# Silu as one activation in place, and the last four transposes of x into halves of two large buffers

## The chip, the cores and the metric

One core of a Trainium2 chip runs the whole program. TensorE (PE) multiplies, VectorE (DVE) and ScalarE (ACT) do the elementwise work, GpSimd (POOL) does almost nothing here, and SyncE (SP) issues nearly all transfers. The metric is the device time of one execution in microseconds (us), lower is better. Three executions of the kernel before give a median of 1471.03 us (1471.02 to 1471.4). The profiled execution took 1471.17 us, of which 1469.4 us lie between its first and its last instruction (the span).

## The reference, cut to what matters

Two decoder layers work on 512 tokens of width 1024, all in f32. One layer is:

```
h = rmsnorm(x);  z = h @ w_in
aq, ak, av, rq, rk, rv, rg, ga, gb = split(z)
ya = sliding_window_attention(aq, ak, av) @ w_a
r  = chunkwise_retention(rq, rk, rv)
r  = r * rsqrt(mean(r * r) + eps)
yb = (r * silu(rg)) @ w_b
x  = x + (sigmoid(ga) * ya + sigmoid(gb) * yb) @ w_out
x  = x + square(relu(rmsnorm(x) @ w_up)) @ w_down
```

A last rmsnorm of x, with its own gain, is the output. Two places of it matter below: silu(rg) = rg * sigmoid(rg), the gate of the retention, and the last `w_down` product with the norm behind it, where the kernel needs x with tokens instead of features on the partitions.

## The kernel before

**Tiling.** x lies in SBUF as eight tiles of 128 features by 512 tokens. Every f32 operand of a product is split into a high and a low part, and a product is three matmuls (hi*hi, hi*lo, lo*hi; `products`, L326), or fewer where two are put side by side. Weights arrive in 336 units of 128x1024 f32 (512 KB) in a fixed order (`unit_order`, L59). SP loads a unit into one of three `raw` buffers (L196), ScalarE writes its high part (L286) and VectorE the low part (L287), into three `hi` and three `lo` buffers. `unit` (L292) has the splits of the next units traced before the products of the present one, so weights are prepared about two units ahead. The last four units of the program go to homes of their own (`homes`, L270 and L525), because they are used until the end.

**Buffers.** Short-lived f32 tiles of 128x512 come from `temp` (L143), with six buffers for all of them. Larger ones of 128x2x512 come from `big` (L146), with seven. A tile waits until one of the buffers of its kind is given back.

**Order.** The Python code traces operations in program order; on leaving its context (L1662) a planner sets each engine's final order once, at build time: it runs a model of the timeline and gives a free engine the first traced operation whose inputs, buffers and semaphores are ready in the model. On the chip each engine, and SP's list of transfers, then runs strictly in that order and waits where something is late. `tc.issue_after(ins)` only keeps the operations in its block behind `ins` on the same engine.

**The retention's gates.** In each layer the eight tiles of rg are `w_in` chunks. `put_rg` (L982) takes a chunk out of PSUM with VectorE, times the norm's factor (L989), into half of a big tile `z`. Then `silu` (L995): ScalarE writes sigmoid(rg) to a temp `sig` (L997), VectorE multiplies it into rg (L998). For tiles 0 to 3 this comes in a block behind the last exponential of the attention, together with two sigmoids on half of the gates ga each (L1141 to L1145); for tiles 4 to 7 it comes from `put_rg` itself (L990). The eight gates gb follow as further chunks (`gate`, L920), with a sigmoid each (L923), while in the background the retention of heads 2 and 3 runs, whose norms take square roots (L454, and L479 for head 3). A head's `finish` (L1084) multiplies z with the norm and with the retention's output.

**The end.** In the last layer, x is turned by `turns` (L509): for each half f of the features, four transposes on VectorE (L516) write a temp `turned` each, SP sends each to DRAM (`blocks`, L517), and after the fourth, four transfers bring x back in the other layout (L520). For f=0 they are spread over the last `w_down` pairs of the third quarter (L1462). For f=1 they stand at the start of `end` (L540), behind the two gain rows `gains`, which hold two of the six temps to the end, and behind two big tiles `x0` for the output. There the products of the last quarter come in two parts. First four banks of PSUM take four units (L548 to L555). Then, for each block of 128 tokens, ScalarE seeds a bank with the turned x of f=1 (`seeded`, L560, copy on L562), TensorE adds the last four units' products on top (L573 to L578), and the norm and the store of that block follow (L579 to L597).

Of the kernel before, what the change touches and what calls it, by code (L numbers as in the profile page):

```python
# [13 lines left out]
AF = mybir.ActivationFunctionType  # L14
ALU = mybir.AluOpType
# [112 lines left out]
def decoder(ctx, tc, xT, x_first, w_in, w_a, w_b, w_out, w_up, w_down, tables, decay, band, triangles, g_last, out):  # L128
    nc = tc.nc
# [13 lines left out]
    def temp(name="t"):  # L143
        return tmp.tile([P, T], F32, tag="t", name=name)

    def big(name, dtype=F32):  # L146
        return tmp.tile([P, 2, T], dtype, tag="big", name=name, bufs=7)
# [361 lines left out]
    def turns(f):  # L509

        four = x[:, 4 * f : 4 * f + 4, :]

        def turn(n):
            new = temp("turned")
            old = four.rearrange("p c (b r j) -> p c b r j", b=NB, j=32)[:, :, :, n, :]
            nc.vector.transpose(new.rearrange("p (b c j) -> p c b j", b=NB, j=32), old)  # L516
            nc.sync.dma_start(blocks[f, :, n, :], new)  # L517
            if n == 3:
                for r in range(4):
                    nc.sync.dma_start(four[32 * r : 32 * r + 32], blocks[f, :, r, :].rearrange("(a p) w -> p a w", a=4))  # L520

        return [partial(turn, n) for n in range(4)]

    def end(layer, uT):
# [14 lines left out]
        with tc.issue_after(last_low[0]):  # L539
            all_of(turns(1))  # L540
# [59 lines left out]
    def layer_body(layer):  # L600
# [379 lines left out]
        rg, rg_next, rg_tiles = {}, {}, {}  # L980

        def put_rg(i):  # L982
            def put(ps):
                if i % 2 == 0:
                    two = rg_tiles[i // 2] = big("z")
                    rg[i], rg_next[i + 1] = two[:, 0, :], two[:, 1, :]
                else:
                    rg[i] = rg_next.pop(i)
                nc.vector.tensor_tensor(rg[i], ps, rstd(), ALU.mult)  # L989
                if i >= 4:  # L990
                    silu(i)

            return put

        def silu(i):  # L995
            s = temp("sig")
            nc.scalar.activation(s, rg[i], AF.Sigmoid)  # L997
            nc.vector.tensor_tensor(rg[i], rg[i], s, ALU.mult)  # L998

        ret = {}  # L1000

# [139 lines left out]
        with tc.issue_after(last_exp[0]):  # L1141
            for hs in (slice(0, T // 2), slice(T // 2, T)):
                nc.scalar.activation(x[:, :, hs], x[:, :, hs], AF.Sigmoid)
            for i in range(4):
                silu(i)  # L1145
# [305 lines left out]
        for what, q, i in mlp_sequence():  # L1451
            if what == "first":
                late = group("w_up", layer, xs, [put_up] * 4, first_hooks())
            elif what == "pair":
                pair(q, i, late)
                if (q, i) == (3, 3):
                    old_input()
                    for t, _ in homes_x:
                        slots.give(*t[1])
            elif what == "down":  # L1460
                if (layer, q, i) == (DEPTH - 1, 2, 2):
                    turning = turns(0)  # L1462
                two_chunks("w_down", layer, up[q], [put_down(2 * i), put_down(2 * i + 1)], turning)
                if i == 3:
                    slots.give(*up_slots[q])
            elif layer == DEPTH - 1:
                end(layer, up[q])
            else:
                new_input()
                all_of(group("w_down", layer, up[q], [put_down(c, True) for c in range(4)]))  # L1470
                for c in range(4, KD):
                    chunk("w_down", layer, up[q], put_down(c, True))
                slots.give(*up_slots[q])
# [193 lines left out]
```

## Time and profile before

| | |
|---|---|
| median of three executions | 1471.03 us |
| profiled execution | 1471.17 us |
| its span | 1469.4 us |
| TensorE busy, by the profile | 1461.8 us |
| VectorE busy | 1171.2 us |
| ScalarE busy | 809.4 us |
| granted TensorE clock | 0.999 |
| moved by DMA | 198.65 MB |

How to read it: "busy" is the union of an engine's instructions. A matmul's end is modelled, and matmuls overlap each other in the pipeline, so a wait of TensorE shows best as a larger distance from one matmul's start to the next one's than in its neighbours. In the groups by line, the columns are line, engine, operation, out<-in with shapes, count, then busy us and mean ns of one, then the idle time of the engine just before them and what ended it. In the waits, the three numbers are the sum in us, how many, and the longest. In the timeline, the columns are start, length, engine, line, operation, tiles, count of merged instructions, and in brackets the idle time before and what ended it. In the table by windows, busy us and count stand for PE, PEld (weight loads of TensorE), DVE, ACT and POOL, then the granted clock, the DMA engines' busy share and GB/s.

### The profile page before, as it was taken

The numbers are of one execution on the slowest core, as the hardware profiler recorded it, in microseconds if no ns is written. First come the engines' busy times: TensorE is split into PE (matmuls) and PEld (weight loads), VectorE is DVE, ScalarE is ACT, GpSimd is POOL, SyncE is SP. The second block draws the span as 40 slices with busy tenths as digits, with TensorE's granted clock in tenths as the row PEclk, the third lists the DMA queues.
The fourth block names the chain that finished last, engine by engine and source line by source line (L and its number), as shares of the span: only waits on it lengthen the run. The fifth ranks groups of instructions, "written<-read, shape, count | busy, mean of one in ns | idle before, by whom it ended". The sixth has DMA issues, their size and how long they took to land.

```text
span 1469.4 us, 20189 instructions
## 1 busy us (share of the span) xinstructions
PE 1461.8 (99%) x7434; PEld 1246.4 (85%) x7434; DVE 1171.2 (80%) x1928; ACT 809.4 (55%) x1302; POOL 3.8 (0%) x14
## 2 busy tenths in 40 slices
PE   9999999999999999999999999999999999999998
PEld 7888888888988888888888888888989888888886
DVE  7998878778988787776678986786899877878773
ACT  7656356654684445444455753656547754444544
POOL 0000000000000000000000000000000000000000
PEclk9999999999999999999999999999999999999999
DMA  6422943256333332333433258333653422333363
GB/s 227 135 87 93 306 147 106 96 173 214 123 127 118 101 115 91 105 106 115 165 123 100 86 182 276 101 104 100 198 186 124 148 96 98 117 101 105 111 197 104
DMA packets 73346, 198.65 MB, mean 135 GB/s; under 512 B 8712, under 2 KB 8864, under 8 KB 73248
## 3 DMA queue, kind: packets, MB, share of 16 engines
q1 hardware_dynamic: 72960, 196.84, 41.1%
q8 instruction: 58, 0.95, 0.3%
q10 hardware_dynamic: 288, 0.52, 0.1%
q14 instruction: 40, 0.33, 0.1%
HBM read 173.73 MB, written 20.98 MB: 133 GB/s over the span
## 4 chain that ended last, share of the span: by engine, by line
PE 94%; issue 5%; DVE 1%; DMA 0%; ACT 0%; POOLq 0%; DVEq 0%; SPq 0%
PE mm L334 22%; PE mm L332 22%; PE mm L333 22%; PE mm L1355 10%; PE mm L1356 5%; PE rv L332 2%; PE rv L334 2%; PE rv L333 2%; PE score L861 1%; PE r L332 1%; PE r L334 1%; PE r L333 1%; PE pT L816 0%; PE pv L843 0%; PE pv L842 0%
## 5 line engine op out<-in xcount | busy, mean ns | idle before, releaser
L333 PE MATMUL mm<-r,hi 128*128 128x512 f32 (+1 forms) x1568 | 572.5, 367 | 0.0
L332 PE MATMUL mm<-r,hi 128*128 128x512 f32 (+1 forms) x1568 | 569.8, 367 | 0.0
L334 PE MATMUL mm<-r,lo 128*128 128x512 f32 (+1 forms) x1568 | 563.9, 367 | 0.2
L286 ACT ACTIVATE hi<-raw 128x1024 fp32r<-128x1024 f32 (+1 forms) x334 | 334.0, 1002 | 385.9 <-PE mm L333 212.7
L287 DVE TENSOR_TENSOR lo<-raw,hi 128x512 fp32r<-128x512 f32 (+1 forms) x335 | 384.3, 1149 | 109.4 <-ACT hi L286 104.0
L334 PEld LDWEIGHTS mm<-r,lo 128*128 128x128 f32 x1568 | 293.6, 188 | 48.6 <-DVE lo L287 1.3
L332 PEld LDWEIGHTS mm<-r,hi 128*128 128x128 f32 x1568 | 294.0, 188 | 46.7 <-ACT r L342 0.4
L333 PEld LDWEIGHTS mm<-r,hi 128*128 128x128 f32 x1568 | 294.3, 188 | 45.9
L1355 PE MATMUL mm<-r,hi 128*128 128x512 f32 x728 | 252.1, 391 | 0.0
L1356 PE MATMUL mm<-r,lo 128*128 128x256 f32 x728 | 200.4, 277 | 0.0
L1355 PEld LDWEIGHTS mm<-r,hi 128*128 128x128 f32 x728 | 136.5, 188 | 28.8 <-ACT mm L1382 0.2
L1356 PEld LDWEIGHTS mm<-r,lo 128*128 128x128 f32 x728 | 136.7, 188 | 3.2 <-DVE lo L287 0.6
L1428 ACT ACTIVATE z<-z 128x512 f32<-128x512 f32 x56 | 32.4, 623 | 49.9 <-DVE z L1408 49.9
L1435 DVE TENSOR_TENSOR x<-x,mm 128x512 f32<-128x512 f32 x56 | 37.7, 685 | 27.7 <-PE mm L334 27.7
L333 PE MATMUL rv<-lo,r 128*128 128x512 f32 x128 | 49.8, 389 | 0.0
L334 PE MATMUL rv<-hi,r 128*128 128x512 f32 x128 | 49.5, 389 | 0.0
L332 PE MATMUL rv<-hi,r 128*128 128x512 f32 x128 | 49.4, 390 | 0.0
L340 DVE TENSOR_TENSOR r<-z,r 128x512 fp32r<-128x512 f32 x64 | 42.7, 684 | 3.0 <-ACT r L339 2.6
L339 ACT ACTIVATE r<-z 128x512 fp32r<-128x512 f32 x64 | 38.2, 618 | 8.0 <-DVE z L1089 8.0
L888 ACT ACTIVATE sm<-sm,st 128x256 f32<-128x256 f32 (+1 forms) x64 | 30.2, 473 | 19.0 <-DVE st L876 18.8
L1408 DVE SCALAR_TENSOR_TENSOR z<-z,rstd 128x512 f32<-128x512 f32 x52 | 35.6, 685 | 0.6
L340 DVE TENSOR_TENSOR r<-sums,r 128x1024 fp32r<-128x1024 f32 x24 | 28.8, 1215 | 0.0
(271 smaller groups left out, 1684.0 us busy)
## 6 DMA issues: line engine op xcount, KB each, us to landing
raw<-w_in_in SPq DMA_DIRECT2D x89, 512.0 KB, 3.6
raw<-w_down_in SPq DMA_DIRECT2D x64, 512.0 KB, 3.5
raw<-w_up_in SPq DMA_DIRECT2D x32, 512.0 KB, 3.5
raw<-w_up_in SPq DMA_DIRECT2D x60, 256.0 KB, 2.8
raw<-w_a_in SPq DMA_DIRECT2D x8, 512.0 KB, 4.8
ahead<-w_b_in SPq DMA_DIRECT2D x8, 512.0 KB, 5.6
park_w_b<-ahead SPq DMA_DIRECT2D x16, 256.0 KB, 5.7
ahead<-w_up_in SPq DMA_DIRECT2D x8, 512.0 KB, 4.6
```

The lines of the kernel that those rows point to most:

```text
L286: nc.scalar.activation(hi[:, at], raw[:, at], AF.Copy)
L287: last_low[:] = [nc.vector.tensor_tensor(lo[:, at], raw[:, at], f32(hi[:, at]), ALU.subtract).ins]
L332: nc.tensor.matmul(ps, ah, bh, start=start and i == 0, stop=False, **more)
L333: nc.tensor.matmul(ps, ah, bl, start=False, stop=False, **more)
L334: nc.tensor.matmul(ps, al, bh, start=False, stop=stop and i == n - 1, **more)
L339: nc.scalar.activation(hi, src, AF.Copy)
L340: nc.vector.tensor_tensor(lo, src, f32(hi), ALU.subtract)
L1355: nc.tensor.matmul(both, hi[:, c], m, start=start and k == 0, stop=False, **more)
L1356: nc.tensor.matmul(ps[:, :H], lo[:, c], m[:, 0, :], start=False, stop=k == 3 and start, **more)
L1408: nc.vector.scalar_tensor_tensor(z[:, :, at], z[:, :, at], 0.0, factor, ALU.max, ALU.mult)
L1428: nc.scalar.activation(z[:, i, :], z[:, i, :], AF.Square)
L1435: nc.vector.tensor_tensor(x[:, c, :], x[:, c, :], ps, ALU.add)
```

## The change

`silu` becomes one activation with the function Silu, reading and writing rg; the temp `sig`, the sigmoid into it and VectorE's product are gone. This concerns eight tiles in each layer.

In `turns`, for f=1 only, the four transposes no longer write four temps but the halves of two big tiles: the first and the third call take a new big tile and use its first half, the second and the fourth use its second half. The transfers are the same, in number, size and program order. For f=0 nothing changes.

```diff
@@ def turns(f):
         four = x[:, 4 * f : 4 * f + 4, :]
+        two = []
 
         def turn(n):
-            new = temp("turned")
+            if f:
+                two[:] = two[1:] or [both[:, i, :] for both in [big("turned")] for i in range(2)]
+            new = two[0] if f else temp("turned")
             old = four.rearrange("p c (b r j) -> p c b r j", b=NB, j=32)[:, :, :, n, :]
             nc.vector.transpose(new.rearrange("p (b c j) -> p c b j", b=NB, j=32), old)
             nc.sync.dma_start(blocks[f, :, n, :], new)
@@ def layer_body(layer):
         def silu(i):
-            s = temp("sig")
-            nc.scalar.activation(s, rg[i], AF.Sigmoid)
-            nc.vector.tensor_tensor(rg[i], rg[i], s, ALU.mult)
+            nc.scalar.activation(rg[i], rg[i], AF.Silu)
```

## The prediction

> **What bounds the kernel now.** The page of the profile comes first: the shares of busy time, then the chain that ended last.
>
> ```profile
> span 1469.4 us, 20189 instructions
> ...
> PE 1461.8 (99%) x7434; PEld 1246.4 (85%) x7434; DVE 1171.2 (80%) x1928; ACT 809.4 (55%) x1302; POOL 3.8 (0%) x14
> ...
> PE 94%; issue 5%; DVE 1%; DMA 0%; ACT 0%; POOLq 0%; DVEq 0%; SPq 0%
> ```
>
> The reader is to see that TensorE is busy for all but 7.6 us of the span and is 94% of the chain. The change takes no matmul away and adds none. Work saved on VectorE is then worth nothing by itself; only a moment in which TensorE waits can be won, and only a new one can be lost. So the next view is the waits of TensorE, of which two are listed in all; this is the one that isn't the start of the program:
>
> ```profile
> PE mm L332 <- ACT mm L562: 0.9, 1, 0.9
> ```
>
> It is at the very end, and the timeline of TensorE there shows it, with one small wait ahead of it:
>
> ```profile
> 1434.52 0.39 PE L334 MATMUL mm<-hi,ulo 128*128 128x512 f32 x1
> 1435.05 0.50 PE L332 MATMUL mm<-hi,r 128*128 128x512 f32 x1
> 1435.38 0.39 PE L333 MATMUL mm<-lo,r 128*128 128x512 f32 x1
> 1435.61 0.40 PE L332 MATMUL mm<-hi,r 128*128 128x512 f32 x1
> ...
> 1439.71 1.07 PE L334 MATMUL mm<-hi,r 128*128 128x512 f32 x4
> 1441.66 0.50 PE L332 MATMUL mm<-r,r 128*128 128x512 f32 x1 [0.88 <-ACT mm L562]
> ```
>
> Undisturbed matmuls start 0.23 us apart (1435.38 to 1435.61). From 1434.52 to 1435.05 are 0.53 us: 0.30 lost. Four from 1439.71 would let the next start at 1439.71 + 4 * 0.23 = 1440.6; it starts at 1441.66: about 1.0 lost, of which the profile counts 0.9 as idle. That is the whole visible prize, under 0.1% of the time.
>
> **Part one, the gates.** These are the rows by line:
>
> ```profile
> L997 ACT ACTIVATE sig<-z 128x512 f32<-128x512 f32 x16 | 9.6, 622 | 0.1
> ...
> L923 ACT ACT_TABLE_LOAD x4 | 5.1, 1283 | 0.1
> ...
> L997 ACT ACT_TABLE_LOAD x2 | 2.6, 1283 | 0.2 <-DVE z L989 0.2
> ```
> ```profile
> L998 DVE TENSOR_TENSOR z<-z,sig 128x512 f32<-128x512 f32 x16 | 10.6, 685 | 3.5 <-ACT sig L997 3.5
> ```
>
> Removed are 16 VectorE products of 685 ns (16 * 0.685 = 11.0 us of VectorE) and 16 temps. The 16 activations stay: the sigmoid takes 622 ns, the kernel's other functions on the same shape nearly the same, so I take 622 for Silu and nothing for the difference. VectorE's 11 us are off the path: credit 0.
>
> What may be added are table loads. A load of 1283 ns stands ahead of a sigmoid that follows a square root. No row shows Silu, so the number of extra loads is bounded from both sides. If Silu shares the sigmoid's table: none. If not: one at each change between sigmoid and Silu that has no load today. ScalarE's order in the first layer shows how many:
>
> ```profile
> 123.53 3.73 ACT L1143 ACTIVATE x<-x 128x2048 f32<-128x2048 f32 x2
> ...
> 130.01 1.14 ACT L997 ACTIVATE sig<-z 128x512 f32<-128x512 f32 x2
> ```
> ```profile
> 276.73 0.62 ACT L997 ACTIVATE sig<-z 128x512 f32<-128x512 f32 x1
> ...
> 279.04 0.61 ACT L923 ACTIVATE gb<-gb 128x512 f32<-128x512 f32 x1
> 279.66 1.28 ACT L454 ACT_TABLE_LOAD   x1
> ...
> 288.47 0.63 ACT L923 ACTIVATE gb<-gb 128x512 f32<-128x512 f32 x1
> ...
> 289.78 0.63 ACT L997 ACTIVATE sig<-z 128x512 f32<-128x512 f32 x1
> ```
>
> Three places: before the gates at 130.01, between the gate at 276.73 and gb at 279.04, and between gb at 288.47 and the gate at 289.78. With the second layer alike that is 6 loads, 6 * 1.283 = 7.7 us of ScalarE; tables that the square roots force are loaded anyway. I take 6, the dear end, because no path depends on it. The cover is ScalarE's own idle time, in windows of which the first holds one such place and the other two one each:
>
> ```profile
> 122.00:150.00 28.00, 28.00 (x129) 23.18 (x128) 22.95 (x40) 19.77 (x25) 0.00 (x0) 1.00 0.43 141
> 250.00:280.00 30.00, 30.00 (x146) 25.51 (x145) 24.85 (x44) 18.50 (x30) 0.00 (x0) 1.00 0.27 90
> 280.00:310.00 30.00, 30.00 (x137) 25.02 (x136) 21.86 (x29) 16.90 (x24) 0.00 (x0) 1.00 0.37 115
> ```
> ```profile
> ACT hi L286 <- PE mm L333: 212.7, 96, 4.5
> ```
>
> ScalarE is idle for 8.2, 11.5 and 13.1 us there while TensorE is busy throughout, and its weight splits sit waiting for TensorE to free a buffer: 2.2 us on average (212.7 / 96). A load of 1.28 us eats into that wait first, and behind it lies the lead of the two prepared units, 24 matmuls of 0.23 us or 5.5 us each. Cost on the path: 0. Without the cover it would be 1.28 us a load, up to 7.7.
>
> The Trainium skill speaks against this part: "ScalarE: Activation LUTs", section "Table sets: the hidden batching unit", says that tables come in named sets, and that a kernel should finish one set's calls before it turns to the next; the sigmoid's set as listed there doesn't name Silu. By its figure of about 2.66 us a switch, drain included, six switches would be 16 us of ScalarE. The trace shows 1283 ns for the load and next to no idle time before it, so the row's figure is the one used above.
>
> **Part two, the last transposes.** VectorE's timeline, then SP's, then ScalarE's:
>
> ```profile
> 1419.90 1.89 DVE L516 STREAM_TRANSPOSE turned<-x 128x512 f32<-128x512 f32 x3
> 1425.72 1.23 DVE L287 TENSOR_TENSOR r<-raw,r 128x1024 fp32r<-128x1024 f32 x1 [3.94 <-ACT r L286]
> ...
> 1429.47 0.70 DVE L516 STREAM_TRANSPOSE turned<-x 128x512 f32<-128x512 f32 x1
> ```
> ```profile
> 1420.79 1.70 SPq L517 DMA_DIRECT2D blocks<-turned  x3
> 1426.98 2.93 SPq L196 DMA_DIRECT2D raw<-w_down_in  x3
> 1430.20 0.33 SPq L517 DMA_DIRECT2D blocks<-turned  x1
> 1430.62 6.13 SPq L520 DMA_DIRECT2D x<-blocks  x4
> ```
> ```profile
> SPq L520 <- DMA blocks<-turned: 4.1, 1, 4.1
> ```
> ```profile
> 1433.41 1.06 ACT L286 ACTIVATE r<-raw 128x1024 fp32r<-128x1024 f32 x1 [0.89 <-DMA raw<-w_down_in]
> 1434.38 1.13 ACT L339 ACTIVATE r<-z 128x512 fp32r<-128x512 f32 x2
> ...
> 1441.00 0.60 ACT L562 ACTIVATE mm<-x 128x512 f32<-128x512 f32 x1 [4.14 <-DMA x<-blocks]
> ```
>
> Three transposes run back to back, then VectorE idles 3.94 us, and the fourth comes only at 1429.47. Six temps explain it: two hold the gains, three the first transposes, one is left for the pair that is still being finished. The fourth's write is issued at 1430.20, behind three weight loads; the last return waits 4.1 us for it; the seed on L562 waits for that return; TensorE waits for the seed. Count the big tiles by the code: two hold a split of the last quarter (`uhi`, `ulo`, which the TensorE rows above still read), one is z, two are x0, and two are left of seven for the transposes, once the last pair's raw tiles are split. So all four should go in a row from 1419.90, the fourth at about 1421.8 instead of 1429.47, beside VectorE's idle 3.94 us. Its write and the four returns move some 7 us forward and past the three weight loads on SP. The seed, today 1.0 us late, is then early; next in line at 1440.6 is the first of the last four weight units, whose split (VectorE's row at 1425.72) is long done. Gain 0.9 us. VectorE's 0.70 us at 1429.47 vanish ahead of z, which may give some of the 0.30 us at 1435.05; I count nothing for it.
>
> **Sum:** 0 for the gates, -0.9 for the end: 1471.17 - 0.9 = 1470.3 us for the profiled execution. The median stands 0.14 us lower than that execution, so 1471.03 - 0.9 = **1470.1 us**.
>
> **The rivals.** *The change doesn't do what it says* (time 1471.0): the big tiles come free too late, or the planner puts the fourth transpose where it was. For it: seven big tiles suffice with none to spare. Against it: by the order of the code the last pair's raw tiles are split before its z is finished, so two are free in time.
>
> *The weights arrive late instead* (slower). The place is ScalarE's order at 1433.41: the split L339, for which TensorE waits at 1435.05, stands behind a weight split that waits for a DMA, with no slack.
>
> ```profile
> blocks<-turned SPq DMA_DIRECT2D x8, 256.0 KB, 2.3
> x<-blocks SPq DMA_DIRECT2D x8, 256.0 KB
> ```
> ```profile
> 1422.00:1427.00 5.00, 5.00 (x24) 4.17 (x23) 1.27 (x2) 2.37 (x4) 0.00 (x0) 1.00 0.83 277
> 1427.00:1430.00 3.00, 3.00 (x15) 2.45 (x15) 3.00 (x4) 0.86 (x1) 0.00 (x0) 1.00 0.72 218
> ```
>
> Five transfers of 256 KB, 1.31 MB, go ahead of the loads. At 218 to 277 GB/s they take 4.7 to 6.0 us; the idle shares there hold 0.17 * 5 + 0.28 * 3 = 1.7 us of that. So the loads come up to 3.0 to 4.3 us later, and TensorE waits as much longer at 1435.05: net +2.1 to +3.4, up to 1474.5 us. It turns slower than before from 0.9 us of push, and by over 0.2% from 3.8. Against it: the planner's model sees the same transfers and can put L339 first. The Trainium skill bears this rival out ("DMA: Bandwidth & Descriptors", section "Queues, rings and completion order"): on each DMA engine, what one issuer sent is consumed in the order of its ring, so early returns are served before later loads. The 4.1 us that the last return waits for a write issued behind three loads agrees.
>
> *The table loads come through*: a retention step on TensorE finds its input late. One to six loads uncovered: 1471.4 to 1477.8 us with the gain of the end. Against it: 8 to 13 us of idle ScalarE in each window.
>
> *The planner lays the engines out anew* from the first changed instruction: TensorE's small waits move, between 1468.6 (all of them gone) and 1474.
>
> **How the numbers follow.** Chances: forecast 0.50; nothing moved 0.15; late weights 0.20, of which 0.04 lie beyond 0.2%; table loads 0.08, of which 0.04; new layout 0.07, of which 0.03 faster and 0.02 slower. 0.2% is 2.9 us, about what a measurement of this kernel can tell from no change: below 1468.1 is faster, above 1474.0 slower. So faster 0.03, slower 0.10, within 0.87. The range from 1469.2 to 1473.2 holds the forecast with all of the 0.30 us too, nothing moved, most of the late weights and the lighter half of the rest: about 0.8.
>
> **What would show it.** Right: four transposes in a row near 1420, no wait of TensorE for L562, no L998, 16 Silu activations of some 620 ns, up to six more table loads, TensorE's count of waits unchanged between 120 and 320 us. Wrong: a fourth transpose late, a longer wait of TensorE for L339 near 1435, or new waits beside a table load.

## The result, and the profile after

The changed kernel takes 1469.18 us (median of 22 runs, 1468.64 to 1470.27) beside 1471.01 us for the kernel before (22 runs on the same chip, 1469.9 to 1472.24). The ratio is 0.9988, with a 95% interval of 0.9983 to 0.9994: 1.8 us (0.12%) faster, and the whole interval lies under 1. The profiled execution's span falls from 1469.4 to 1467.5 us.

The page after, the lines that answer to those of before (lines of the kernel stand up to three further down now: the transposes are L519, the seed is L565, Silu is L999, the gates gb are L926):

```profile
span 1467.5 us, 20166 instructions
...
PE 1461.0 (100%) x7434; PEld 1246.4 (85%) x7434; DVE 1161.6 (79%) x1912; ACT 814.6 (56%) x1306; POOL 3.7 (0%) x14
...
PE 99%; DVE 0%; issue 0%; POOLq 0%; ACT 0%; DVEq 0%; ACTq 0%
```

TensorE has the same 7434 matmuls. VectorE has lost 9.6 us of work with its 16 products, ScalarE has gained 5.2 us. What the span lost is time in which TensorE waited, as the sum at the end of this section shows. The waits of TensorE after are one line, the start of the program:

```profile
PE warm L311 <- DVE ones L306: 1.0, 1, 1.0
```

So the wait for the seed is gone. The timeline of TensorE at both places of before, 1435.05 and 1441.66 there, shows that the small one is gone too:

```profile
1434.31 0.39 PE L334 MATMUL mm<-hi,ulo 128*128 128x512 f32 x1
1434.54 0.39 PE L332 MATMUL mm<-hi,r 128*128 128x512 f32 x1
...
1439.75 0.39 PE L334 MATMUL mm<-hi,r 128*128 128x512 f32 x1
1439.98 0.39 PE L332 MATMUL mm<-r,r 128*128 128x512 f32 x1
```

The first use of the last split (from `ulo` to `r`) and the first use of the late units (`r,r`) both follow at the usual 0.23 us. VectorE, SP and ScalarE there, in this order:

```profile
1419.16 2.48 DVE L519 STREAM_TRANSPOSE turned<-x 128x512 f32<-128x512 f32 x4
1421.57 0.65 DVE L1409 SCALAR_TENSOR_TENSOR z<-z,rstd 128x512 f32<-128x512 f32 x1
```
```profile
1419.89 2.42 SPq L520 DMA_DIRECT2D blocks<-turned  x4
1422.36 1.36 SPq L531 DMA_DIRECT2D gains<-g_last_in  x2
1425.56 1.41 SPq L523 DMA_DIRECT2D x<-blocks  x3
1427.06 0.39 SPq L196 DMA_DIRECT2D raw<-w_down_in  x1
1427.49 0.43 SPq L523 DMA_DIRECT2D x<-blocks  x1
1428.19 1.82 SPq L196 DMA_DIRECT2D raw<-w_down_in  x2
```
```profile
1431.33 1.14 ACT L339 ACTIVATE r<-z 128x512 fp32r<-128x512 f32 x2
1435.28 1.06 ACT L286 ACTIVATE r<-raw 128x1024 fp32r<-128x1024 f32 x1 [2.81 <-DMA raw<-w_down_in]
1436.96 0.60 ACT L565 ACTIVATE mm<-x 128x512 f32<-128x512 f32 x1 [0.63 <-DMA x<-blocks]
1437.95 1.06 ACT L286 ACTIVATE r<-raw 128x1024 fp32r<-128x1024 f32 x1 [0.39 <-DMA raw<-w_down_in]
1439.18 1.06 ACT L286 ACTIVATE r<-raw 128x1024 fp32r<-128x1024 f32 x1 [0.16 <-DMA raw<-w_down_in]
```

Four transposes run in a row. The gain rows now come behind their writes. Three returns precede the weight loads and the fourth goes among them. The seed runs at 1436.96 instead of 1441.00. The price is in the weights: their last three splits on ScalarE began at 1430.42, 1433.41 and 1435.80 before and begin at 1435.28, 1437.95 and 1439.18 now, 4.9, 4.5 and 3.4 us later. TensorE doesn't feel it (no distance behind 1400 us is more than 0.01 us over the usual one), because the split it needs first (L339) is now ahead of them at 1431.33, where it was behind two of them at 1434.38.

The gates, by line on ScalarE:

```profile
L999 ACT ACTIVATE z<-z 128x512 f32<-128x512 f32 x16 | 9.6, 628 | 3.3 <-DVE z L992 3.2
L926 ACT ACT_TABLE_LOAD x6 | 7.7, 1283 | 0.1
L999 ACT ACT_TABLE_LOAD x4 | 5.1, 1283 | 0.1
```

Silu takes 628 ns where the sigmoid took 622. It does not share the sigmoid's table: loads at these two lines go from 4 + 2 to 6 + 4, the program's from 19 to 23.

To place the gain, I took from the trace, for every matmul that starts after 1400 us, the distance to the matmul before, less the usual distance for their two widths (227 ns for 512 behind 512). The sum is the time lost there: 1.85 us before, 0.16 us after. This is 1.7 us, of 1.8 by the medians and 1.9 by the two spans. Nearly all of it before lies at the two places: 0.30 and 1.04 us at the two late matmuls, and 0.1 us more at the matmul behind each of them, which is late too, 0.33 us behind the one ahead of it. For the second place the row of before is this one, behind the 1441.66 of the prediction:

```profile
1441.99 0.39 PE L333 MATMUL mm<-r,r 128*128 128x512 f32 x1
```

### The profile page after: what moved, and what is told of

Same layout as the page of the kernel before. It is cut to its first block, busy times and chain, and to the rows that moved or that the text cites. A ratio compares the mean times of both kernels' runs of the same rounds, so it can differ in the third digit from the quotient of the medians.

```text
span 1467.5 us, 20166 instructions
## 1 busy us (share of the span) xinstructions
PE 1461.0 (100%) x7434; PEld 1246.4 (85%) x7434; DVE 1161.6 (79%) x1912; ACT 814.6 (56%) x1306; POOL 3.7 (0%) x14
## 4 chain that ended last, share of the span: by engine, by line
PE 99%; DVE 0%; issue 0%; POOLq 0%; ACT 0%; DVEq 0%; ACTq 0%
PE mm L334 24%; PE mm L332 23%; PE mm L333 23%; PE mm L1356 11%; PE mm L1357 6%; PE rv L332 2%; PE rv L334 2%; PE rv L333 2%; PE score L864 1%; PE r L332 1%; PE r L334 1%; PE r L333 1%; PE pT L819 0%; PE pv L846 0%; PE pv L845 0%; PE warm L311 0%
## 5 line engine op out<-in xcount | busy, mean ns | idle before, releaser
L333 PE MATMUL mm<-r,hi 128*128 128x512 f32 (+1 forms) x1568 | 572.5, 367 | 0.0
L334 PE MATMUL mm<-r,lo 128*128 128x512 f32 (+1 forms) x1568 | 563.9, 367 | 0.2
L287 DVE TENSOR_TENSOR lo<-raw,hi 128x512 fp32r<-128x512 f32 (+1 forms) x335 | 384.3, 1150 | 110.8 <-ACT hi L286 109.4
L334 PEld LDWEIGHTS mm<-r,lo 128*128 128x128 f32 x1568 | 293.6, 188 | 48.8 <-DVE lo L287 1.4
L333 PEld LDWEIGHTS mm<-r,hi 128*128 128x128 f32 x1568 | 294.3, 188 | 46.0
L334 PE MATMUL rv<-hi,r 128*128 128x512 f32 x128 | 49.8, 389 | 0.0
L333 PE MATMUL rv<-lo,r 128*128 128x512 f32 x128 | 49.8, 389 | 0.0
L339 ACT ACTIVATE r<-z 128x512 fp32r<-128x512 f32 x64 | 38.5, 619 | 16.3 <-DVE z L1090 16.1
L340 DVE TENSOR_TENSOR r<-z,r 128x512 fp32r<-128x512 f32 x64 | 42.9, 685 | 4.7 <-ACT r L339 4.3
L340 DVE TENSOR_TENSOR r<-sums,r 128x1024 fp32r<-128x1024 f32 x24 | 28.9, 1216 | 0.0
```

The lines of the kernel that those rows point to most:

```text
L287: last_low[:] = [nc.vector.tensor_tensor(lo[:, at], raw[:, at], f32(hi[:, at]), ALU.subtract).ins]
L333: nc.tensor.matmul(ps, ah, bl, start=False, stop=False, **more)
L334: nc.tensor.matmul(ps, al, bh, start=False, stop=stop and i == n - 1, **more)
L339: nc.scalar.activation(hi, src, AF.Copy)
L340: nc.vector.tensor_tensor(lo, src, f32(hi), ALU.subtract)
```

## The experiments

The runs come in three groups, each on one chip and with the kernel before beside it: at a median of 1470.82 us in the first group (33 runs), 1470.6 in the second (32) and 1471.13 in the third (15). Ratios are to before in the same group; the medians of two groups don't compare directly. The first group has Silu alone, turns alone, gains in a big tile and the split behind the weights; the third has the two rows marked so; the rest is in the second. "Lost at the end" is the sum just described, in the one profiled execution.

| kernel | median us | ratio to before | 95% interval | lost at the end, us |
|---|---|---|---|---|
| Silu alone | 1470.59 | 0.9999 | 0.9990 to 1.0008 | 1.59 |
| turns alone | 1469.82 | 0.9993 | 0.9984 to 1.0002 | 0.18 |
| turns alone, again | 1469.37 | 0.9990 | 0.9981 to 0.9999 | 0.18 |
| gains in a big tile | 1469.73 | 0.9992 | 0.9983 to 1.0001 | 0.17 |
| changed, again | 1468.96 | 0.9988 | 0.9979 to 0.9997 | 0.18 |
| changed, product kept | 1469.48 | 0.9990 | 0.9981 to 0.9999 | 0.20 |
| split behind the weights | 1474.51 | 1.0026 | 1.0017 to 1.0035 | 5.64 |
| the same, in order on TensorE (third group) | 1476.68 | 1.0039 | 1.0025 to 1.0053 | 9.40 |
| a root before every other Silu (third group) | 1471.16 | 1.0001 | 0.9992 to 1.0010 | 0.23 |
| a root before each Silu | 1474.42 | 1.0026 | 1.0016 to 1.0035 | 0.26 |

**My theory** was that the end alone gives the gain: the fourth transpose no longer waits for a temp, and the gates cost and give nothing on the path. **Rival A**: the gates give part of it (lighter VectorE, free temps). **Rival B**: table loads reach the path, and the change would be faster without them. **Rival C**: the planner's new layout of the whole program makes the difference.

**Silu alone.** Edit to the kernel before:

```diff
-            s = temp("sig")
-            nc.scalar.activation(s, rg[i], AF.Sigmoid)
-            nc.vector.tensor_tensor(rg[i], rg[i], s, ALU.mult)
+            nc.scalar.activation(rg[i], rg[i], AF.Silu)
```

> The kernel before with the Silu activation alone; the last transposes stay in temps. My theory (the whole gain is at the end): the time of before within 0.4 us, 16 products of 685 ns gone from VectorE, about 4 more table loads than before, and TensorE's two late waits (0.3 and 1.0 us, near 1435 and 1441 us) still there. Rival A (the gates give the gain, by 11 us less on VectorE or by temps that come free): 1.0 to 1.8 us faster. Rival B (table loads reach the path): 1 to 5 us slower.

No difference from before is measured, with the same 23 table loads as the changed kernel. The waits of TensorE keep both late places, and VectorE still has the fourth transpose apart:

```profile
PE mm L332 <- ACT r L339: 0.6, 1, 0.6
PE mm L332 <- ACT mm L562: 0.2, 1, 0.2
```
```profile
1419.93 1.90 DVE L516 STREAM_TRANSPOSE turned<-x 128x512 f32<-128x512 f32 x3
1430.26 0.70 DVE L516 STREAM_TRANSPOSE turned<-x 128x512 f32<-128x512 f32 x1
```

Their sizes have moved against each other: the wait for L339, too short for the list before, is now 0.6, and the wait for the seed 0.2 instead of 0.9. What is lost at the end falls little, from 1.85 to 1.59 us. A and B get no support.

**Turns alone.** The other half of the diff, with sigmoid and product kept.

> The kernel before with the last four transposes in halves of two big tiles; the gates keep sigmoid and product. My theory: the whole gain, 1.5 to 1.9 us faster than before, both late waits of TensorE gone. Rival A (the gates give it): within 0.4 us of before. Rival C (a new layout of the whole program by the planner): the gain is not there with either part alone, or the waits go elsewhere.

> The turns alone once more, beside the changed kernel on one chip. My theory: the changed kernel's time within 0.3 us, and a first phase of slow matmuls of another length than in the first profile of this kernel (it was the longest of all, up to 7 us), since its length is chance. Rival A: 0.5 us or more slower than the changed kernel, with the same long first phase.

The end loses 0.18 us, as in the changed kernel: all of the gain there comes with this part. The medians say it less sharply: 1.0 us under before in the first group, where the interval still holds no change, and 1.2 us in the second, where it just doesn't. Both are less than the 1.5 to 1.9 us that I expected, with intervals of about 2.6 us in width. The changed kernel beside it on the same chip:

> The changed kernel as it is, on the same chip as the turns alone, to see whether the Silu activation adds to their gain. My theory: it adds nothing, 1.0 to 1.9 us faster than before. Rival A: 0.5 us or more faster than the turns alone. The spread of single runs should come from the first microseconds, in which the matmuls start 0.43 us apart and not 0.23: between 11 and 15 of them do, from run to run.

It is 0.4 us faster than the turns alone by the medians, a little more than the 0.3 that I allowed, with intervals that overlap almost whole. The traces show no place for such a difference: after the first 100 us the losses of TensorE sum to 8.7 us in this profile of the changed kernel, 9.0 in its first, and 8.9 in the second profile of the turns alone (9.5 in its first). That the Silu adds something under 0.5 us can't be excluded by these runs.

**The gains in a big tile.** One edit to the kernel before, which gives the temps back in another way:

```diff
-        gains = [temp("gains") for _ in range(2)]
+        both_gains = big("gains")
+        gains = [both_gains[:, f, :] for f in range(2)]
```

> The kernel before with one edit: the two gain rows of the end lie in the halves of one big tile, so two temps more are free, and the transposes stay in temps. My theory (the fourth transpose waits for a temp, six being too few): four transposes in a row near 1420 us, the wait of TensorE for the seed gone, 1.0 to 1.8 us faster than before. Rival (the big tile as target, or the planner's layout, makes the difference): the fourth transpose stays at about 1429 us and the time within 0.3 us of before.

VectorE's timeline has the four in a row, into temps as before:

```profile
1420.85 2.49 DVE L516 STREAM_TRANSPOSE turned<-x 128x512 f32<-128x512 f32 x4
```

The end loses 0.17 us. The median falls by 1.1 us, as expected, though the interval still holds no change; the trace is what decides here. So it was the shortage of temps that held the fourth transpose, as the prediction had read it, and not something in the target tile. Rival C gets no support either: two different edits, each with a plan of its own, win the same 1.7 us at the same place. Elsewhere a gain or loss by the plan under some 0.6 us can't be excluded: between 100 and 1400 us two profiles of the same kernel, the turns alone, differ by that much (9.3 and 8.8 us lost).

**The product kept.** The changed kernel, with this behind the Silu (its result is not used):

```diff
             nc.scalar.activation(rg[i], rg[i], AF.Silu)
+            s = temp("sig")
+            nc.vector.tensor_tensor(s, rg[i], rg[i], ALU.mult)
```

> The changed kernel with VectorE's product kept, as a square of the gate into a temp that nobody reads: VectorE has its 11 us of work and the 16 temps back. My theory (VectorE's work is off the path): the time of the changed kernel within 0.4 us, and no late wait of TensorE at the end. Rival A (the lighter VectorE gives part of the gain): 0.5 to 1 us slower than the changed kernel.

VectorE is back at 1171.2 us of work. The median is 0.5 us over the changed kernel's on the same chip, outside the 0.4 that I expected and at the lower edge of rival A; single runs of the two overlap (1468.66 to 1470.38 and 1468.70 to 1469.47), so the medians don't settle it. The traces speak against A: the waits at the end stay gone, TensorE loses 8.4 us after the first 100 us where the changed kernel loses 8.7, and the span is 0.1 us longer (1467.2 to 1467.1). VectorE's 11 us have no place on the path that the trace shows.

**The split behind the weights.** In the changed kernel, the last pair's split of z is put behind the weight split of the third late unit, where it stood before (of the edit, the lines that place it):

```diff
+            if u == 2:
+                with tc.issue_after(last_high[0]):
+                    held.pop()()
```

Here `held` has the splits of z, on ScalarE and VectorE (L339 and L340 in the changed kernel), and `last_high` is the last weight split on ScalarE.

> The changed kernel with the last pair's split of z put behind the weight split of the third of the last four units on ScalarE, the place it had before. My theory (the weights do come 3 to 5 us later now, and only ScalarE's new order keeps TensorE from waiting): TensorE waits 4 to 5 us for that split near 1435 us, 1473 to 1474 us. Rival (the loads would have come in time if something waited for them): a wait of at most 1 us, under 1470.3 us.

3.7 us slower than before, so some 5.5 us slower than the changed kernel, which is more than I expected and did not come in the way I had meant. TensorE's timeline (products L333 to L335, seed L569 in this kernel) shows that it waited for a seed: seeing the split late, the planner had put the second part of the products (`r,r`) first.

```profile
1434.19 0.39 PE L335 MATMUL mm<-hi,ulo 128*128 128x512 f32 x1
1438.11 0.50 PE L333 MATMUL mm<-r,r 128*128 128x512 f32 x1 [3.53 <-ACT mm L569]
1438.45 0.40 PE L334 MATMUL mm<-r,r 128*128 128x512 f32 x1
1438.69 0.52 PE L335 MATMUL mm<-r,r 128*128 128x512 f32 x1
1439.01 0.63 PE L333 MATMUL mm<-r,r 128*128 128x512 f32 x1
1439.43 0.63 PE L334 MATMUL mm<-r,r 128*128 128x512 f32 x1
```

A second kernel therefore holds TensorE's order as well (`first_part` is the last matmul of the first part; again only the lines that place it):

```diff
-                multiply(ps, k, b, units[k // 2], False, False, True, at)
+                with tc.issue_after(first_part):
+                    multiply(ps, k, b, units[k // 2], False, False, True, at)
```

> The kernel of the run before on this question (the last split of z behind the third of the four late weight splits on ScalarE), with TensorE's second part of the last products held behind its first part, as the changed kernel has it; the planner had swapped them there, so that TensorE waited for the seed and not for the split. My theory: TensorE waits for that split from about 1434.5 to 1439.5 us, 4.5 to 5 us, and then runs its matmuls 0.43 us apart for some 3 us as it did after the other wait; 1474.5 to 1476.5 us. Rival (the split was not what the order protects): a wait of at most 1 us, under 1471 us.

TensorE, then ScalarE (here the products are L334 to L336, weight splits L287 and the split of z L342):

```profile
1434.01 0.39 PE L336 MATMUL mm<-hi,ulo 128*128 128x512 f32 x1
1440.57 0.79 PE L334 MATMUL mm<-hi,r 128*128 128x512 f32 x1 [6.17 <-ACT r L342]
1441.16 0.63 PE L335 MATMUL mm<-lo,r 128*128 128x512 f32 x1
1441.58 0.63 PE L334 MATMUL mm<-hi,r 128*128 128x512 f32 x1
...
1446.28 0.43 PE L335 MATMUL mm<-lo,r 128*128 128x512 f32 x1
1446.54 0.39 PE L334 MATMUL mm<-hi,r 128*128 128x512 f32 x1
```
```profile
1436.36 1.06 ACT L287 ACTIVATE r<-raw 128x1024 fp32r<-128x1024 f32 x1 [5.69 <-DMA raw<-w_down_in]
...
1438.94 1.06 ACT L287 ACTIVATE r<-raw 128x1024 fp32r<-128x1024 f32 x1 [0.41 <-DMA raw<-w_down_in]
1439.90 1.13 ACT L342 ACTIVATE r<-z 128x512 fp32r<-128x512 f32 x2
```

This is the rival of the late weights as the prediction described it, with the wait at the named place: 6.2 us, and behind it another 2.8 us, because the matmuls start 0.43 us apart until 1446.28. The median is 0.4% over before, and 0.2 us over the range that I expected. The profiled execution is the slowest of the four (1478.2 us, the others 1476.1 to 1477.2), and in it the second and third weight splits begin about 1.0 us later than in the changed kernel (1438.94 to 1437.95 for the third), so part of the 6.2 us is that. The rest comes of the place of the split of z in ScalarE's order; having it ahead of the late weights is what keeps the changed kernel from this wait.

**Table loads.** The changed kernel, with this ahead of each Silu (the root is not used):

```diff
+            root = small.tile([P, 1], F32, tag="root", name="root", bufs=1)
+            nc.scalar.activation(root, rg[i][:, 0:1], AF.Square)
+            nc.scalar.activation(root, root, AF.Sqrt)
             nc.scalar.activation(rg[i], rg[i], AF.Silu)
```

> The changed kernel with a square root of one column of the gate ahead of each of the 16 Silu activations (its result is not used), so that ScalarE has to load the square root's table and then Silu's again: up to 32 loads more, 41 us of ScalarE. My theory (ScalarE's idle time and the two prepared weight units cover loads): within 1 us of the changed kernel, 1468.5 to 1470.5 us. Rival B (loads reach the path, and the changed kernel escapes only because it has few): 1.3 us for each that does, 5 to 40 us slower.

It has 49 loads instead of 23, 26 more, and is 5.4 us slower than the changed kernel (1474.42 to 1468.96 on the same chip). This is outside what I expected: the cover is not as deep as I had said. Rival B's 1.3 us a load is wrong too; the mean is 0.2. (The next expectation counts 24 loads more, two too few.) The 32 small activations of the roots, 0.2 us each, come on top of the loads and are not told apart from them here. TensorE's waits after the start, the larger ones (`ssq` is the bank of the square sums, `rv` and `pv` are products for the retention's values and of the attention):

```profile
PE ssq L450 <- DVE sh L340: 1.3, 2, 0.7
PE rv L333 <- DVE lo L287: 1.2, 1, 1.2
...
PE rv L332 <- DVE rot L699: 0.7, 1, 0.7
```

> The changed kernel with a square root of one column ahead of every other Silu activation: about half the extra table loads of the run that had one ahead of each (24 more, 5.4 us over the changed kernel's 1469.0). My theory (a margin that is used up: loads are free until ScalarE's results come later than the lead of the prepared work): clearly less than half of the 5.4 us, 1469.0 to 1471 us. Rival (each load costs its share, 0.22 us): 1471.3 to 1472.2 us.

Twelve more loads than in the changed kernel (35). The medians don't settle this one. 1471.16 us lies between the two ranges, and the group as a whole ran 0.5 us slower than the one with the 1469.0. Against before, each in its own group, this kernel stands at 0.0, the changed one at -1.6 and the one with all roots at +3.8: 1.7 us for 12 loads and 5.5 us for 26, or 0.14 and 0.21 us a load, with intervals too wide to tell the theories apart. The timeline of TensorE shows where the loss comes from, two waits, both behind the first layer's attention:

```profile
141.61 0.73 PE L845 MATMUL pv<-r,r 128*128 128x512 f32 x2 [0.73 <-ACT r L339]
161.17 0.50 PE L333 MATMUL rv<-lo,r 128*128 128x512 f32 x1 [0.45 <-DVE lo L287]
```

The four stretches with gates, two in each layer, have these table loads and these losses of TensorE, in us, by the sum of distances:

| stretch, us | before | changed | every other | each |
|---|---|---|---|---|
| 115 to 165 | 1 load, 0.15 | 2, 0.12 | 6, 1.89 | 9, 1.75 |
| 240 to 325 | 5, 0.59 | 6, 0.55 | 8, 0.55 | 12, 1.70 |
| 835 to 885 | 1, 0.20 | 2, 0.20 | 6, 0.21 | 9, 1.26 |
| 960 to 1050 | 5, 0.53 | 6, 0.54 | 8, 0.54 | 12, 1.64 |

The second column answers rival B: where the changed kernel makes its four loads more, TensorE loses no more than before. Beyond that, cover is a matter of place and not of a price by the load. Six loads behind the first layer's attention cost 1.8 us and nine there cost no more, while six behind the second layer's cost nothing. What in ScalarE's order makes the two layers differ is not shown.

## Why the prediction was right in its direction and low in its size

- **TensorE bounds the kernel, and only its waits can be won.** Right: same matmuls, span shorter by what TensorE waited less.
- **The gates: credit 0, up to 6 loads more, cost 0.** Right for this change: 4 loads came, since the planner now runs the last two gates of each layer before the first gb, so that one of the three alternations vanished; TensorE loses nothing at them, and Silu alone measures as no change. The reason was too general, and that the term held owes something to luck: the cover as I gave it, idle microseconds per window and two units of lead everywhere, would have made the roots free as well, and behind the first layer's attention four loads more than the changed kernel makes are felt. Idle time of an engine in a window doesn't say that it is idle at the moment that counts.
- **The fourth transpose waits for a temp, and with big tiles it goes at once.** Right, shown by the two ways of giving the temps back.
- **Gain at the end 0.9 us.** This is the step that was mis-sized: the end gave 1.7 us. I took the 0.9 us that the list of waits shows and counted nothing for the 0.30 us at 1435.05. The first wait costs 1.04 us by the distances and the second goes wholly, as its row had suggested; and the matmul behind each late one comes late as well (1435.05 to 1435.38 and 1441.66 to 1441.99 are 0.33 us, not 0.23). 1.04 + 0.30 + 2 * 0.10 = 1.5 us could have been read from the rows of before; all but the last of them stand in the prediction. What moved the 0.30 us is not the transpose that vanished from VectorE, where I had looked for it, but ScalarE's order: L339 runs ahead of the late weights now.
- **Late weights.** The rival's mechanism is there and its size was about right (3.4 to 4.9 us later, 3.0 to 4.3 foretold). The reason given against it decided: the planner's order has L339 first. That both can be true at once, the push and the gain, was foreseen only as an either-or. Its price was put too low: with the old place of L339 the wait was 6.2 us, not 3.0 to 4.3, and the 2.8 us of slow matmuls after it were not in the sum.
- **The range.** 1469.18 lies at its lower edge, 1469.2, because the forecast left out half of the gain.

## What to carry to other kernels

When one engine is busy all the time, measure its waits by the distance between starts, not by the list of waits: small waits and the late matmul behind each wait are missing from the list, and here they were half of the prize. A buffer kind that is one short showed here as a run of equal operations that broke off while its engine went idle; giving buffers back from either side (larger tiles for the writer, or for a long-lived holder) cured it. When a step moves ahead, look at what its transfers push back, and whether anything that the bound engine needs stands behind those on an in-order engine.

## What the runs showed of the hardware

**Matmuls at half rate.** At the start the matmuls are 0.43 us apart and then 0.23. The phase counts 8 to 14 such distances in the ten profiles of the experiments (11 to 15 in the expectation above) and ends between 4.6 and 7.2 us, also for one kernel: 13 of them, until 7.0 us, in the first profile of the turns alone, and 12, until 6.4 us, in the second. By the sum of distances the first 100 us lose 2.9 to 3.9 us in these profiles. This is a part of the spread of a kernel's times, but not the whole, as I had thought: the two profiles of the turns alone differ by 1.1 us, 0.6 of it in the first 100 us and 0.6 between 100 and 1400 us; the two of the changed kernel differ by 0.5 us, 0.1 of it in the first 100 us.

The same pace came back after the waits of 3.5 and 6.2 us, and not after those of 1.2 us or less. There the granted clock shows it. These are stretches of the run with the wait of 3.5 us, with the clock third from the end:

```profile
1436.00:1438.00 2.00, 0.00 (x0) 0.00 (x0) 0.97 (x1) 1.54 (x2) 0.00 (x0) 1.00 0.88 325
1438.00:1440.00 2.00, 1.89 (x6) 1.50 (x7) 0.82 (x2) 1.72 (x4) 0.00 (x0) 0.70 0.07 29
1440.00:1442.00 2.00, 2.00 (x7) 1.54 (x6) 2.00 (x4) 1.39 (x2) 0.00 (x0) 0.50 0.00 0
1442.00:1444.00 2.00, 2.00 (x10) 1.65 (x9) 1.00 (x1) 0.00 (x0) 0.00 (x0) 0.94 0.00 0
```

In this run the clock falls to half only at 1438.8, when TensorE has begun again (at 1438.11; the next matmuls still start 0.34 and 0.24 us apart), and it stays there for 3.4 us by the trace's record. In the run with the wait of 6.2 us it falls at 1439.5, a microsecond before TensorE goes on, and stays for 6.8 us. For the first microseconds of the program the record says 1.00, although the matmuls are 0.43 us apart there.

The Trainium skill, "TensorE: Matmul & The Clock Gate", section on the HAM clock gate, puts this down to a clock gate that is at half rate until a free-running activity window of about 3.4 us has been busy, and again after an idle one, and notes that the count at the start varies from run to run. The traces agree: the count varies between profiles of one kernel, the slow pace does not return after 1.2 us and does after 3.5 us, and after the waits the half clock lasts one and two times 3.4 us.

**Silu and the sigmoid don't share a table.** In the changed kernel a load of 1283 ns stands at each change from sigmoid to Silu and from Silu to sigmoid, four more in all than before. Silu doesn't share the square root's table either: with a root ahead of each, all 16 Silu activations have a load of 1283 ns of their own.
